# A decoder block on one core: TensorE's order in the recurrence heads written out by hand

## The chip, the cores and the metric

The kernel runs on one core of a Trainium2 chip. The metric is the time of one execution on the device in microseconds (us); a measurement is a median over several runs. The engines are TensorE (PE, with its weight loads shown apart as PEld), VectorE (DVE), ScalarE (ACT), GpSimd (POOL) and SyncE (SP), which here only issues transfers.

## What is computed

One decoder block over 1024 tokens of width 1024, all in float32. A projection gives seven parts; a gated recurrence (HGRN2, 8 heads of 128 by 128, chunks of 16 tokens in the reference) and a causal pooling over 2, 4, 8 and 16 tokens run side by side, are gated and added; then come a layer norm, an MLP with squared ReLU and a second layer norm.

```
proj = x @ w_in -> [q | f | i | og | pool_v | gate_a | gate_b]
f = lb + (1 - lb) * sigmoid(f);  k = 1 - f;  q = silu(q) / sqrt(128)
S_t = diag(f_t) S_{t-1} + k_t v_t^T;   o_t = S_t^T q_t          (v = i, per head)
a = (rms_norm(o) * g * sigmoid(og)) @ w_a
b = (causal_mean_w(pool_v) - pool_v) @ w_pool * pool_scale       (per group)
x = LN(alpha * x + (sigmoid(gate_a) * a + sigmoid(gate_b) * b) @ w_out)
x = LN(alpha * x + relu(x @ w_up)^2 @ w_down)
```

## The kernel before

Every large product runs in Strassen's manner: a pair of 128-column blocks of weights for both halves of the tokens takes seven products (p1 to p7) on sums of operands. Each operand is split into a high and a low part of type fp32r, and a product is 12 matmuls of 128x512 (`prod`, lines 201, 203 and 204). `pair` builds the seven steps, `run` goes through them: for each step it makes the weights' parts (a copy on ACT, line 118, and a subtraction on DVE, line 119, into the ring `w` of ten tiles, two for each operand), then calls the product, which drains its bank in PSUM through `takes`.

The stage of the heads follows the projection of `i` (the values). Its pairs are:

- `head_inputs(h)`, q and f of head h, kept on chip in the rings `q` and `f`;
- `output_gates(h)` (two heads at a time), stored to DRAM and loaded back as `og`;
- `pooled(g)`, whose means DVE makes in the drains, stored to DRAM (`pod`);
- `gates(j)`, eight of them, stored to DRAM (`gad`, `gbd`).

`pool_products(g)` then loads the pooled tiles back (`pod` into the tags `og` and `v`), splits them and multiplies them by `w_pool` (`mm3`, lines 105 to 107), 24 matmuls each.

The recurrence works on 16 halves: 8 heads, each with two halves of 512 tokens, a half being four chunks of 128 tokens. `hgrn(h, u, ...)` does a half. DVE scans the running products of f in blocks of 16 (`fd`, line 811), takes their reciprocal (line 817) and makes scaled queries and keys (`qc`, `kc`, `kr`, `q64`, `k64`, `qi`, `ke`). PE turns the keys (`ke`, line 870), multiplies them with the values (`ds`, line 875), from which DVE makes the states one after the other (`st`, line 883). PE makes the scores in pieces of 32 and 64 (lines 887 and 898) into the bank `sc`; DVE masks them into `att` (line 905). PE multiplies `att` with the values and `qi` with the states into `o` (lines 915 and 918). ACT squares, takes the root and scales (lines 923 to 928), PE turns the result (line 931), DVE multiplies it by the output gate (line 932) and SP's queue stores it to DRAM (`od`, line 933). `o_sums(kp)` loads four such tiles, makes the four Strassen sums and stores them.

A planner orders the instructions of each engine: it simulates a timeline and takes, on each engine, the ready instruction that was written earliest, or that stands in a block of raised priority. So PE's order in the heads comes from the plan: the narrow products of the recurrence lie wherever the plan had them ready, between the 512-wide products of the pairs. The trace order in which heads and pairs are written is the loop over `h` and `u` with the table `EXTRAS`. Every load and almost every store of the stage is issued by SP, in one queue.

Tags are rings of buffers: a tile waits until the tile that had its buffer is released, stores to DRAM included. Before, the rings are `q`=3, `f`=3, `og`=2, `v`=2, `tA`=2, `tC`=2, `st`=2, the others 1.

After `pool_products` and the last `gates`, the merged stage (`a_pair`), the output projection, the norm and the MLP follow; the change doesn't touch them.

Of the kernel before, what the change touches and what calls it, by code (L numbers as in the profile page):

```python
# [16 lines left out]
P = 128  # L17
# [12 lines left out]
PRIO_LAST = 3000  # L30
# [13 lines left out]
def tile_hybrid_block(  # L44
# [311 lines left out]

    def run(*pairs, made=(), behind=()):


        for i, steps in enumerate(zip(*pairs)):  # L360
            made_now = list(made[i]) if made else []
            if made_now:
                made_now.pop(0)()
            with tc.issue_after(made_last[behind[i]]) if behind and behind[i] else nullcontext():
                ws = [{operand: operand() for operand in operands} for operands, _ in steps]
            for n in range(len(ws[0])):
                if made_now:
                    made_now.pop(0)()
                for w, (_, products) in zip(ws, steps):
                    operand, product = products[n]  # L370
                    product(w[operand])

# [219 lines left out]
    def loaded(src, tile_of):  # L592
        t = tile_of()
        nc.sync.dma_start(out=t, in_=src)
        return t
# [9 lines left out]
    def o_sums(kp, tile_of=c_tile):  # L605

        a11, a21, a12, a22 = (loaded(od[k][u], tile_of) for k, u in ((kp, 0), (kp, 1), (kp + CH, 0), (kp + CH, 1)))
# [4 lines left out]
        for name, t in zip(("s3", "s2", "s1", "s4"), (a21, a11, a22, a12)):  # L612
            nc.sync.dma_start(out=osd[name][kp], in_=t)
# [4 lines left out]
    with tc.tile_pool(name="tmp", bufs=1, side="right", reuse_waits="tile") as tmp:  # L618
# [3 lines left out]
        att = [hgp.tile([P, CH, P], F32, name=f"att{i}") for i in range(1)]  # L622
        for t in att:
            G.memset(t, 0.0)
# [6 lines left out]
        RINGS = dict(q=3, f=3, og=2, v=2, tA=2, tC=2, st=2)  # L631
# [11 lines left out]
        def head_inputs(h, behind=()):  # L643
            fs, qs = [None, None], [None, None]
# [23 lines left out]
            return fs, qs  # L668
# [19 lines left out]
        def gates(j):  # L688
# [3 lines left out]
            def take(dst, src=None, more=None):  # L692
                def put(t):
# [5 lines left out]
                    nc.sync.dma_start(out=dst if more is None else more, in_=s)  # L699
# [8 lines left out]
        def pool_products(g):  # L708
# [6 lines left out]
            raw = raw_tile().rearrange("p k n c -> p (k n c)")[:, : 2 * 2 * P].rearrange("p (k c) -> p k c", c=2 * P)  # L715
            nc.sync.dma_start(out=raw, in_=w_pool[g].rearrange("(k p) c -> p k c", p=P))
            wh, wl = split(raw, lambda: room(F32R).rearrange("p (k c) -> p k c", c=2 * P))
            for u in range(2):
                pl = [split(loaded(pod[2 * g + i][u], room), row_tile) for i in range(2)]
                for i in range(2):  # L720
# [9 lines left out]
                    nc.sync.dma_start(out=pbd[j][u], in_=t)  # L730

        def pooled(g):
# [20 lines left out]
            def put(c, i, u):  # L753
                nc.sync.dma_start(out=pod[j + i][u], in_=c[:, HALO:])
# [51 lines left out]
        def hgrn(h, u, ft, q, v, og, state):  # L806

            fd = tt("tA")
            for i in range(2):
                w = slice(i * QUARTER, (i + 1) * QUARTER)  # L810
                V.tensor_tensor_scan(fd[:, w], starts.rearrange("p b s -> p (b s)"), ft[:, w], 1.0, ALU.max, ALU.mult)
            k = ft
            A.activation(k, ft, AF.Identity, bias=cmask[:, P - 1 : P], scale=-1.0)
            r = tt("tC")
            for i in range(CH):
                w = slice(i * P, (i + 1) * P)
                V.reciprocal(r[:, w], fd[:, w])  # L817
            T = small("T", [P, NB])
            G.tensor_copy(T, blk(fd)[:, :, SUB - 1])
            T2 = T.rearrange("p (b e) -> p b e", e=2)  # L820
            p32 = small("p32", [P, CH, 4])
            p32f = p32.rearrange("p c b -> p (c b)")
            G.tensor_mul(p32f, T2[:, :, 0], T2[:, :, 1])
            p64 = small("p64", [P, CH, 2])
            p32p = p32f.rearrange("p (b e) -> p b e", e=2)
            G.tensor_mul(p64.rearrange("p c e -> p (c e)"), p32p[:, :, 0], p32p[:, :, 1])
            dec = small("dec", [P, CH])
            G.tensor_mul(dec, p64[:, :, 0], p64[:, :, 1])
            eq = small("eq", [P, CH, 4])
            G.memset(eq[:, :, 0:1], 1.0)  # L830
            G.tensor_copy(eq[:, :, 1], p32[:, :, 0])
            G.tensor_copy(eq[:, :, 2], p64[:, :, 0])
            G.tensor_mul(eq[:, :, 3], p64[:, :, 0], p32[:, :, 2])
            ek = small("ek", [P, CH, 4])
            G.memset(ek[:, :, 3:4], 1.0)
            G.tensor_copy(ek[:, :, 2], p32[:, :, 3])
            G.tensor_copy(ek[:, :, 1], p64[:, :, 1])
            G.tensor_mul(ek[:, :, 0], p64[:, :, 1], p32[:, :, 1])


            V.tensor_mul(q, q, fd)
            kc = tt("tD")
            V.tensor_mul(kc, k, r)
            kr = tt("tE")
            V.tensor_mul(blk(kr), blk(kc), bc(T, [P, NB, SUB]))
            A.copy(pairs_of(kc)[:, :, 0], pairs_of(kr)[:, :, 0])
            qc = tt("tF")
            A.copy(pairs_of(qc)[:, :, 1], pairs_of(q)[:, :, 1])
            V.tensor_mul(
                pairs_of(qc)[:, :, 0], pairs_of(q)[:, :, 0],  # L850
                bc(pairs_of(r)[:, :, 0, SUB - 1], [P, NB // 2, SUB]),
            )
            V.tensor_mul(pairs_of(q)[:, :, 1], pairs_of(q)[:, :, 1], bc(T2[:, :, 0], [P, NB // 2, SUB]))
            V.tensor_mul(pairs_of(kr)[:, :, 0], pairs_of(kr)[:, :, 0], bc(T2[:, :, 1], [P, NB // 2, SUB]))
            q64 = hgp.tile([P, CH, 2, 32], F32, tag="q64", name=nm("q64"))
            k64 = hgp.tile([P, CH, 2, 32], F32, tag="k64", name=nm("k64"))
            A.copy(q64[:, :, 0], half64(q, 1)[:, :, 0])
            V.tensor_mul(q64[:, :, 1], half64(q, 1)[:, :, 1], bc(p32[:, :, 2], [P, CH, 32]))
            A.copy(k64[:, :, 1], half64(kr, 0)[:, :, 1])
            V.tensor_mul(k64[:, :, 0], half64(kr, 0)[:, :, 0], bc(p32[:, :, 1], [P, CH, 32]))  # L860
            qi = tt("tA")
            b32 = lambda t: t.rearrange("p (b s) -> p b s", s=32)
            V.tensor_mul(b32(qi), b32(q), bc(eq.rearrange("p c b -> p (c b)"), [P, 16, 32]))
            ke = tt("tC")
            V.tensor_mul(b32(ke), b32(kr), bc(ek.rearrange("p c b -> p (c b)"), [P, 16, 32]))


            pt = ps_tile("tr", 2)
            for c in range(CH - u):
                PE.transpose(pt[:, c * P : (c + 1) * P], ke[:, c * P : (c + 1) * P], ident)  # L870
            ket = tt("tH")
            A.copy(ket[:, : (CH - u) * P], pt[:, : (CH - u) * P])
            ds = ps_tile("hg", 2)
            for c in range(CH - u):
                PE.matmul(ds[:, c * P : (c + 1) * P], ket[:, c * P : (c + 1) * P], v[:, c], start=True, stop=True)
            st = tt("st")
            for c in range(CH - u):
                o = st[:, c * P : (c + 1) * P]
                if state is None and c == 0:
                    V.tensor_copy(o, ds[:, 0:P])  # L880
                else:
                    prev = state[:, 3 * P :] if c == 0 else st[:, (c - 1) * P : c * P]
                    V.scalar_tensor_tensor(o, prev, dec[:, c : c + 1], ds[:, c * P : (c + 1) * P], ALU.mult, ALU.add)


            def score(part, lo, keys, queries):
                PE.matmul(sc[part : part + 32, lo : lo + queries.shape[-1]], keys, queries, start=True, stop=True)

            for c in range(CH):
                for b in range(4):  # L890
                    lo = c * P + b * 32
                    score(b * 32, lo, kc[:, lo : lo + 32], qc[:, lo : lo + 32])
            for c in range(CH):
                for b in (0, 2):
                    lo = c * P + b * 32
                    score(b * 32, lo + 32, kr[:, lo : lo + 32], q[:, lo + 32 : lo + 64])
            for c in range(CH):
                PE.matmul(
                    sc[0:64, c * P + 64 : (c + 1) * P],
                    k64[:, c].rearrange("p a b -> p (a b)"),  # L900
                    q64[:, c].rearrange("p a b -> p (a b)"),
                    start=True, stop=True,
                )
            at = att[(2 * h + u) % 1]
            V.copy_predicated(
                at, cmask.bitcast(U32).unsqueeze(1).to_broadcast([P, CH, P]),
                sc.rearrange("p (c t) -> p c t", t=P),
            )


            o = ps_tile("hg", 2)
            for c in range(CH):
                w = slice(c * P, (c + 1) * P)
                first = state is None and c == 0
                PE.matmul(o[:, w], at[:, c], v[:, c], start=True, stop=first)
                if not first:
# [485 lines left out]
```

## Time and profile before

| | before |
|---|---|
| median of 3 runs | 1462.83 us (1462.3 to 1464.97) |
| profiled execution | 1460.19 us, of which the span from the first to the last instruction is 1458.5 us |
| mean granted PE clock | 0.996 |
| matmuls | 7377 |
| HBM | 154.16 MB read, 71.30 MB written, 155 GB/s over the span |

The heads stretch from about 107 us to about 650 us of the span. In the profile's rows, "<-" behind an idle time names what ended it; a line number is that of the kernel; an engine's name with a "q" behind it stands for the queue that issues transfers. [...]

### The profile page before, as it was taken

To read this page: it belongs to the slowest core of one execution; us is meant where nothing else is said; L and a number is where in the kernel's file an instruction comes from. 1 tells how busy PE (TensorE), PEld (TensorE's weight loads), DVE (VectorE), ACT (ScalarE), POOL (GpSimd) and SP (SyncE) were. 2 spreads that over 40 slices of the span, in tenths; PEclk is the share of its full clock that TensorE was granted. 3 is DMA by queue.
4 is the path that set the end of the run, shared out by engine and by line. 5 is a ranking of instruction groups with operands and counts; after the bars stand their busy time and mean duration, and the time that the engine had idled before them with its cause. 6 is when DMAs were issued, how large, how long until landed. Compare 5 with 4: busy or idle time off the path is not lost.

```text
span 1458.5 us, 20662 instructions
## 1 busy us (share of the span) xinstructions
PE 1436.4 (98%) x7377; PEld 1187.9 (81%) x7377; DVE 1141.6 (78%) x1838; ACT 758.3 (52%) x1383; POOL 58.6 (4%) x244
## 2 busy tenths in 40 slices
PE   8999999999999998999999999999999999999997
PEld 7888888888888886788888878888888888888886
DVE  5967989899898885768985597666666787777977
ACT  5445565666656655556542376555555443333535
POOL 0001001001000010000002100000000100000000
PEclk9999999999999999999999999999999999999999
DMA  7232233323234447897672225444474874445322
GB/s 253 70 126 87 85 98 101 109 75 114 90 99 138 152 132 249 301 299 241 223 247 99 73 94 195 159 146 144 152 261 149 275 260 150 153 141 163 130 73 116
DMA packets 160615, 226.82 MB, mean 156 GB/s; under 512 B 11232, under 2 KB 84480, under 8 KB 160512
## 3 DMA queue, kind: packets, MB, share of 16 engines
q1 hardware_dynamic: 158576, 218.93, 44.7%
q0 software_dynamic: 1152, 4.19, 0.8%
q10 hardware_dynamic: 784, 2.38, 0.5%
q8 instruction: 58, 0.95, 0.3%
q14 instruction: 45, 0.37, 0.1%
HBM read 154.16 MB, written 71.30 MB: 155 GB/s over the span
## 4 chain that ended last, share of the span: by engine, by line
PE 94%; DVE 3%; DMA 1%; ACT 1%; issue 0%; SPq 0%; DVEq 0%
PE ps_pj L201 16%; PE ps_pj L203 16%; PE ps_pj L204 16%; PE ps_pj L1283 4%; PE ps_pj L1285 4%; PE ps_pj L1284 4%; PE ps_pj L106 3%; PE ps_pj L107 3%; PE ps_pj L105 2%; PE ps_tr L1285 1%; PE ps_tr L1283 1%; PE ps_tr L1284 1%; PE ps_sc L201 1%; PE ps_sc L203 1%; PE ps_sc L204 1%; PE ps_hg L203 1%
## 5 line engine op out<-in xcount | busy, mean ns | idle before, releaser
L201 PE MATMUL ps_pj<-act,w 128*128 128x512 f32 x1068 | 421.6, 395 | 0.4 <-ACT act L123 0.2
L203 PE MATMUL ps_pj<-act,w 128*128 128x512 f32 x1068 | 415.1, 390 | 0.5 <-DVE act L124 0.5
L204 PE MATMUL ps_pj<-act,w 128*128 128x512 f32 x1068 | 414.1, 390 | 0.0
L201 PEld LDWEIGHTS ps_pj<-act,w 128*128 128x128 f32 x1068 | 200.6, 188 | 42.8 <-ACT act L123 0.6
L204 PEld LDWEIGHTS ps_pj<-act,w 128*128 128x128 f32 x1068 | 200.5, 188 | 42.3
L203 PEld LDWEIGHTS ps_pj<-act,w 128*128 128x128 f32 x1068 | 200.6, 188 | 40.6 <-DVE act L124 0.9
L118 ACT CAST w<-t 128x512 fp32r<-128x512 f32 x170 | 104.7, 620 | 105.0 <-PE ps_pj L203 53.8
L118 ACT CAST w<-raw 128x512 fp32r<-128x512 f32 x143 | 88.2, 620 | 117.3 <-PE ps_pj L203 62.5
L119 DVE TENSOR_TENSOR w<-raw,w 128x512 fp32r<-128x512 f32 x143 | 99.8, 702 | 55.2 <-ACT w L118 53.9
L119 DVE TENSOR_TENSOR w<-t,w 128x512 fp32r<-128x512 f32 x170 | 115.9, 685 | 29.6 <-ACT w L118 29.4
L1245 ACT CAST act<-act 128x1024 fp32r<-128x1024 f32 x66 | 66.9, 1050 | 107.9 <-issue 35.0
L1246 DVE TENSOR_TENSOR act<-act,act 128x1024 fp32r<-128x1024 f32 x66 | 79.3, 1220 | 18.5 <-ACT act L1245 15.8
L1285 PE MATMUL ps_pj<-act,act 128*128 128x512 f32 x240 | 92.9, 389 | 0.0
L1284 PE MATMUL ps_pj<-act,act 128*128 128x512 f32 x240 | 92.9, 389 | 0.0
L1283 PE MATMUL ps_pj<-act,act 128*128 128x512 f32 x240 | 92.4, 389 | 0.0
L275 DVE TENSOR_TENSOR c<-c,ps_pj 128x512 f32<-128x512 f32 x95 | 64.5, 681 | 18.0 <-PE ps_pj L204 13.4
L271 ACT COPY c<-ps_pj 128x512 f32<-128x512 f32 x96 | 55.2, 582 | 12.8 <-PE ps_pj L204 12.8
L817 DVE RECIPROCAL tC<-tA 128x128 f32<-128x128 f32 x64 | 54.1, 904 | 0.0
L1284 PEld LDWEIGHTS ps_pj<-act,act 128*128 128x128 f32 x240 | 45.1, 188 | 9.4
L1285 PEld LDWEIGHTS ps_pj<-act,act 128*128 128x128 f32 x240 | 45.1, 188 | 9.4
L1283 PEld LDWEIGHTS ps_pj<-act,act 128*128 128x128 f32 x240 | 45.1, 188 | 9.3
L241 DVE TENSOR_TENSOR t<-raw,raw 128x512 f32<-128x512 f32 x43 | 29.6, 689 | 21.9 <-DMA raw<-in_w_in_dram 19.7
(415 smaller groups left out, 2719.8 us busy)
## 6 DMA issues: line engine op xcount, KB each, us to landing
h<-c SPq DMA_DIRECT2D x106, 256.0 KB, 2.1
act<-h SPq DMA_DIRECT2D x78, 256.0 KB, 2.9
raw<-in_w_in_dram SPq DMA_DIRECT2D x64, 256.0 KB, 3.4
draw<-in_w_down_dram SPq DMA_DIRECT2D x16, 1024.0 KB, 7.8
raw<-in_w_up_dram SPq DMA_DIRECT2D x30, 512.0 KB, 4.2
raw<-in_w_in_dram SPq DMA_DIRECT2D x18, 512.0 KB, 4.0
hf<-h SPq DMA_DIRECT2D x34, 256.0 KB, 2.9
c<-o SPq DMA_DIRECT2D x24, 256.0 KB, 3.4
```

The source lines that it names most:

```text
L118: A.copy(hi, src)
L119: V.tensor_sub(lo, src, f(hi))
L201: PE.matmul(ps, wh[:, k], th, start=first and k == 0, stop=False, skip_group_check=True)
L203: PE.matmul(ps, wh[:, k], tl, start=False, stop=False, skip_group_check=True)
L204: PE.matmul(ps, wl[:, k], th, start=False, stop=k == CH - 1, skip_group_check=True)
L271: A.copy(t, ps)
L275: V.tensor_add(t, t, ps)
L1245: A.copy(hi, src)
L1246: V.tensor_sub(lo, src, f(hi))
L1283: PE.matmul(ps, hh[:, w], wh, start=fresh and n == 0, stop=False, skip_group_check=True)
L1284: PE.matmul(ps, hh[:, w], wl, start=False, stop=False, skip_group_check=True)
L1285: PE.matmul(ps, hl[:, w], wh, start=False, stop=n == M - 1, skip_group_check=True)
```

## The change

1. All products on PE from the first `output_gates` to the last `gates` stand in a block in which PE keeps the order in which they are written (`manual_schedule` for PE). The other engines are planned as before.
2. The recurrence is rewritten as a class `Half` with its pieces and a generator `recurrence()`, which `run` advances by one turn after each product of a pair. A half gets 8.5 turns. Its narrow products stand in two groups: at a half's first turn the outputs of the half before (`outputs`), the turning of its own keys and all its scores (`turn_keys`, `scores`); four turns later the turning of the outputs of the half before and its own states (`turn_outputs`, `states`). `prepare` (DVE's and ACT's work for the next half) is spread over the other turns. The table `ORDER` replaces `EXTRAS`: 147 products from `output_gates(0)` to `gates(5)`, behind them the turns that are left, then `pool_products(0)`, `gates(6)`, `pool_products` 1, 2 and 3, `gates(7)`.
3. In `prepare` the reciprocal of all 512 running products goes; instead two scans that run backwards over f give the products to the end of a block, and the reciprocal is taken of the 32 block ends alone.
4. Stores of `gates` and `output_gates` go to ACT's queue; stores of the outputs, of the pooled tiles, of `pool_products`, and loads and stores of `o_sums`, go to POOL's.
5. Rings: `og` 2 to 1, `tC` 2 to 1, `f` 3 to 4, `tH` 1 to 2. The weights of `w_pool` are loaded into `tA` and no longer into the ring of the large weights. `o_sums` follow the last half of a head in the recurrence.

The diff, cut to its core:

```diff
-PRIO_LAST = 3000
+PER_HALF = 8.5
+TURN_BACK = 4
+TURNS_AHEAD = 3
+ORDER = (
+    ("inputs", 1), ("pooled", 0), ("inputs", 2), ("gates", 0), ("output_gates", 2), ("inputs", 3), ("pooled", 1),
+    ("inputs", 4), ("output_gates", 4), ("gates", 1), ("inputs", 5), ("pooled", 2), ("inputs", 6), ("output_gates", 6),
+    ("gates", 2), ("inputs", 7), ("pooled", 3), ("gates", 3), ("gates", 4), ("gates", 5),
+)
...
     def run(*pairs, made=(), behind=()):
...
                     product(w[operand])
+                    next(turning[0], None)
...
     def o_sums(kp, tile_of=c_tile):
-        a11, a21, a12, a22 = (loaded(od[k][u], tile_of) for k, u in ((kp, 0), (kp, 1), (kp + CH, 0), (kp + CH, 1)))
+        a11, a21, a12, a22 = (loaded(od[k][u], tile_of, nc.gpsimd) for k, u in ((kp, 0), (kp, 1), (kp + CH, 0), (kp + CH, 1)))
...
-            nc.sync.dma_start(out=osd[name][kp], in_=t)
+            nc.gpsimd.dma_start(out=osd[name][kp], in_=t)
...
-        RINGS = dict(q=3, f=3, og=2, v=2, tA=2, tC=2, st=2)
+        RINGS = dict(q=3, f=4, og=1, v=2, tA=2, tH=2, st=2)
...
-                    nc.sync.dma_start(out=dst, in_=s)
+                    nc.scalar.dma_start(out=dst, in_=s)
...
-                    nc.sync.dma_start(out=dst if more is None else more, in_=s)
+                    (nc.scalar if more is None else nc.gpsimd).dma_start(out=dst if more is None else more, in_=s)
...
-            raw = raw_tile().rearrange("p k n c -> p (k n c)")[:, : 2 * 2 * P].rearrange("p (k c) -> p k c", c=2 * P)
+            raw = tt("tA").rearrange("p (k c) -> p k c", c=2 * P)
...
-                    nc.sync.dma_start(out=pbd[j][u], in_=t)
+                    nc.gpsimd.dma_start(out=pbd[j][u], in_=t)
...
-                nc.sync.dma_start(out=pod[j + i][u], in_=c[:, HALO:])
+                nc.gpsimd.dma_start(out=pod[j + i][u], in_=c[:, HALO:])
...
+            def prepare(self):
+                h, u = self.h, self.u
+                ft, q = inputs[h][0][u], inputs[h][1][u]
+                fd = tt("tA")
+                for i in range(2):
+                    w = slice(i * QUARTER, (i + 1) * QUARTER)
+                    V.tensor_tensor_scan(fd[:, w], first_of, ft[:, w], 1.0, ALU.max, ALU.mult)
+                to_end = tt("tC")
+                G.memset(to_end[:, HALF - 1 :], 1.0)
+                yield
+                V.tensor_tensor_scan(
+                    to_end[:, HALF - 2 : QUARTER - 1 : -1], ft[:, HALF - 1 : QUARTER : -1], first_of[:, 1:],
+                    1.0, ALU.mult, ALU.max,
+                )
+                V.tensor_tensor_scan(
+                    to_end[:, QUARTER - 1 :: -1], ft[:, QUARTER : 0 : -1], first_of, 0.0, ALU.mult, ALU.max,
+                )
+                k = ft
+                A.activation(k, ft, AF.Identity, bias=cmask[:, P - 1 : P], scale=-1.0)
+                rT = small("rT", [P, NB])
+                V.reciprocal(rT, blk(fd)[:, :, SUB - 1])
...
+                yield
+                V.tensor_mul(q, q, fd)
+                self.kr = kr = tt("tE")
+                V.tensor_mul(kr, k, to_end)
+                yield
...
+            def outputs(self):
+                self.og = loaded(ogd[self.h][self.u], lambda: tt("og"))
+                o = ps_tile("hg", 2)
...
+            def turn_outputs(self):
+                pt = ps_tile("tr", 2)
+                for c in range(CH):
+                    PE.transpose(pt[:, chunk(c)], self.on[:, chunk(c)], ident)
+                V.scalar_tensor_tensor(self.og, pt, g_col[:, self.h : self.h + 1], self.og, ALU.mult, ALU.mult)
+                nc.gpsimd.dma_start(out=od[self.h][self.u], in_=self.og)
+
+        def recurrence():
...
+            now, old, at = half(0, None), None, 0.0
+            now.load()
+            for _ in now.prepare():
+                yield
+            for _ in range(TURNS_AHEAD):
+                yield
+            for n in range(2 * HEADS + 1):
+                if old:
+                    old.outputs()
+                if now:
+                    now.turn_keys()
+                    now.scores()
+                yield
+                if now:
+                    now.far_queries()
+                nxt = half(n + 1, now) if now else None
+                pieces = nxt.prepare() if nxt else iter(())
+                at += PER_HALF
+                for turn in range(1, round(at) - round(at - PER_HALF)):
+                    if turn == TURN_BACK:
+                        if old:
+                            old.turn_outputs()
+                        if now:
+                            now.states()
+                        if nxt:
+                            nxt.load()
+                        if old and old.u and old.h >= CH:
+                            last = old.h == HEADS - 1
+                            tags = iter(("tD", "tE", "tF", "tC"))
+                            o_sums(old.h - CH, (lambda: tt(next(tags))) if last else c_tile)
+                    else:
+                        next(pieces, None)
+                    yield
+                for _ in pieces:
+                    pass
+                now, old = nxt, now
+
+        inputs = [None] * HEADS
+        head_inputs(0, (None, None, "p6", None, None))
+        with tc.manual_schedule(engines={mybir.EngineType.PE}):
+            turns = turning[0] = recurrence()
+            output_gates(0)
+            for what, j in ORDER:
...
+            for _ in turns:
+                pass
+            for what, j in (
+                ("pool_products", 0), ("gates", 6), ("pool_products", 1), ("pool_products", 2), ("pool_products", 3), ("gates", 7),
+            ):
+                dict(gates=gates, pool_products=pool_products)[what](j)
```

More of the change, by code (lines that the diff above doesn't have):

```diff
@@ L621, in tile_hybrid_block @@
         G.memset(starts[:, :, 0:1], 1.0)
-        att = [hgp.tile([P, CH, P], F32, name=f"att{i}") for i in range(1)]
-        for t in att:
-            G.memset(t, 0.0)
+        att = hgp.tile([P, CH, P], F32, name="att")
+        G.memset(att, 0.0)
         hg_tags.remove("sc")
@@ L804, in bc @@
             return a.unsqueeze(len(a.shape)).to_broadcast(shape)
[L806 to L880, printed above, removed]
-                else:
[L882 to L916, printed above, removed]
-                    prev = state[:, 3 * P :] if c == 0 else st[:, (c - 1) * P : c * P]
-                    PE.matmul(o[:, w], qi[:, w], prev, start=False, stop=True)
-            ss = small("ss", [P, CH])
-            on = tt("tH")
-            for c in range(CH):
-                w = slice(c * P, (c + 1) * P)
-                A.activation(on[:, w], o[:, w], AF.Square, accum_out=ss[:, c : c + 1])
-            A.activation(ss, ss, AF.Sqrt, bias=eps_rms, scale=1.0 / P)
-            V.reciprocal(ss, ss)
-            for c in range(CH):
-                w = slice(c * P, (c + 1) * P)
-                A.activation(on[:, w], o[:, w], AF.Copy, scale=ss[:, c : c + 1])
-            pt = ps_tile("tr", 2)
-            for c in range(CH):
-                PE.transpose(pt[:, c * P : (c + 1) * P], on[:, c * P : (c + 1) * P], ident)
-            V.scalar_tensor_tensor(og, pt, g_col[:, h : h + 1], og, ALU.mult, ALU.mult)
-            nc.sync.dma_start(out=od[h][u], in_=og)
-            return st
@@ L946, in tile_hybrid_block, with chunk @@
[L946 to L962 removed]
+        def chunk(c):
+            return slice(c * P, (c + 1) * P)
```

149 lines of the change are left out of this document (119 added, 30 removed).

## The prediction

> **What bounds the kernel now.** I read the page first, then what TensorE (PE) waits for, then stage windows and the timeline of the one place where it stops.
>
> ```profile
> span 1458.5 us, 20662 instructions
> PE 1436.4 (98%) x7377; PEld 1187.9 (81%) x7377; DVE 1141.6 (78%) x1838; ACT 758.3 (52%) x1383; POOL 58.6 (4%) x244
> PE 94%; DVE 3%; DMA 1%; ACT 1%; issue 0%; SPq 0%; DVEq 0%
> ...
> PE ps_pj L105 <- ACT w L118: 4.7, 1, 4.7
> ...
> PE ps_hg L915 <- DVE st L883: 1.2, 1, 1.2
> PE ps_pj L106 <- DVE w L119: 0.8, 1, 0.8
> ...
> 300.00:350.00 50.00, 50.00 (x348) 41.72 (x347) 48.96 (x100) 33.24 (x76) 4.50 (x26) 1.00 0.30 95
> 550.00:600.00 50.00, 43.25 (x252) 34.83 (x252) 28.76 (x52) 24.34 (x57) 0.00 (x0) 0.93 0.77 254
> ```
>
> PE is busy for 98% of the span and carries 94% of the chain. In the heads (about 107 to 650 us) it never stops before 575 us, though VectorE (DVE) is full at 48.96 of 50 us in the worst window. So nothing that makes DVE, ScalarE (ACT) or a queue faster is worth anything there by itself. Two things can be won: PE time spent on breaks between kinds of product, and the hole near 580 us.
>
> ```profile
> 574.10 0.83 PE L875 MATMUL ps_hg<-v,tH 128*128 128x128 f32 x6
> 577.80 0.39 PE L918 MATMUL ps_hg<-st,tA 128*128 128x128 f32 x2
> 582.85 1.22 PE L105 MATMUL ps_pj<-w,q 128*128 128x512 f32 x2 [4.66 <-ACT w L118]
> 591.31 0.40 PE L107 MATMUL ps_pj<-w,f 128*128 128x512 f32 x1
> 592.45 0.39 PE L201 MATMUL ps_pj<-act,w 128*128 128x512 f32 x1
> ...
> 582.80:586.00 3.20, 3.11 (x7) 1.95 (x8) 1.57 (x3) 3.13 (x7) 0.00 (x0) 0.50 0.78 265
> 586.00:589.40 3.40, 3.40 (x13) 2.62 (x12) 1.24 (x2) 2.80 (x5) 0.00 (x0) 0.61 0.30 77
> ```
>
> Five 512-wide products start between 591.31 and 592.45: 0.227 us each at full clock. From 574.10 to 582.85 PE had 2.5 us of work in 8.75, so 6.2 us are lost. From 582.85 to 592.45 it ran 22 such products and four transposes, 5.4 us of work in 9.6: 4.2 us lost, 0.8 of them a wait, some 3.3 to the granted clock (0.50, then 0.61). **The hole costs 10.4 us.** [...]
>
> **The change, part by part.**
>
> *Groups.* The timeline gives what narrow products cost, as the time between the 512-wide rows around them less the two 0.227 us that those take.
>
> ```profile
> 137.96 0.38 PE L887 MATMUL sc<-tF,tD 128*32 128x32 f32 x18
> ...
> 588.71 0.49 PE L931 MATMUL ps_tr<-ident,tH 128*128 128x128 f32 x3
> ...
> 436.20 0.39 PE L204 MATMUL ps_pj<-act,w 128*128 128x512 f32 x1
> 436.43 0.60 PE L931 MATMUL ps_tr<-ident,tH 128*128 128x128 f32 x4
> 437.53 0.40 PE L203 MATMUL ps_pj<-act,w 128*128 128x512 f32 x1
> ...
> 442.53 0.40 PE L204 MATMUL ps_pj<-act,w 128*128 128x512 f32 x1
> 442.76 1.05 PE L875 MATMUL ps_hg<-v,tH 128*128 128x128 f32 x8
> 445.35 0.39 PE L203 MATMUL ps_pj<-act,w 128*128 128x512 f32 x1
> ...
> 450.36 0.39 PE L204 MATMUL ps_pj<-act,w 128*128 128x512 f32 x1
> 450.58 0.60 PE L915 MATMUL ps_hg<-v,att 128*128 128x128 f32 x4
> 452.38 0.40 PE L203 MATMUL ps_pj<-act,w 128*128 128x512 f32 x1
> ```
>
> Here one half's work stands nearly whole: both transposes 0.88, states with all scores 2.37, outputs 1.57: 4.81 us. Second halves turn one chunk less, first halves have one product fewer, which makes 76.3 us for 16 whole halves. Added up in this way, the 67 interruptions of before (first and last shown) come to 81.4 us without the hole. The surplus is breaks inside the scores. Two whole groups per half: **−5.1 us**. Nothing else of PE's work changes: no product is added or removed.
>
> *DVE and ACT in `prepare`.*
>
> ```profile
> L817 DVE RECIPROCAL tC<-tA 128x128 f32<-128x128 f32 x64 | 54.1, 904 | 0.0
> L811 DVE TENSOR_TENSOR_SCAN tA<-starts,f 128x256 f32<-128x256 f32 x32 | 20.3, 672 | 1.1 <-PE ps_hg L918 1.1
> L843 DVE TENSOR_TENSOR tD<-f,tC 128x512 f32<-128x512 f32 x16 | 10.9, 683 | 0.0
> ...
> ACT w L118 <- PE ps_pj L203: 56.6, 43, 4.3
> ```
>
> Each half loses four reciprocals (3.6 us) and one 512-wide multiplication (0.7); it gains two scans (1.3), half a multiplication and a small reciprocal (about 0.6 as I estimate): about −2.4 us, 38 us in all. PE never waited for DVE in the heads, so I count it at 0; it is the slack that the fixed order lives on.
>
> *The written order.* PE can no longer step past a product whose operand is late; behind it every later product queues. ACT's wait for L203 says that weight parts are made as early as PE frees their buffers, so in steady state they are ready. The drains keep their 2.7 us (12 products) between two products of a pair. Before, waits outside the hole were near 0; the only late recurrence operand cost 1.2 us. Between 0 and 10 us over 34 groups I take **+3 us**, near the low end.
>
> *Stores on ACT's and GpSimd's (POOL's) queues.* SP's queue loses some 130 stores; nobody on PE waited for SP outside the hole, so 0. ACT gets about 46 issues, POOL about 80, on an engine busy for 4%; what they queue behind is the gate's sigmoid on ACT and the small decay products on POOL, which have a half's time.
>
> *The hole.* The last half's outputs now come after the fifth of the seven products of `gates(5)`; its way back (`turn_outputs`) falls behind the last product, and the next thing in PE's order is `pool_products(0)`. Its first operand is a pooled tile loaded into tag `og`, a ring that goes from two buffers to one: the load waits until the last half's own output is stored. `gates(6)`, which could fill the time, is written behind. So the hole stays. Its chain:
>
> ```profile
> 565.13 0.28 ACT L923 ACTIVATE tH<-ps_hg 128x128 f32<-128x128 f32 x1 [0.93 <-PE ps_hg L918]
> 566.29 1.28 ACT L924 ACT_TABLE_LOAD   x1
> 569.99 1.14 ACT L928 ACTIVATE tH<-ps_hg,ss 128x128 f32<-128x128 f32 x4 [2.10 <-DVE ss L925]
> 571.55 0.75 DVE L932 SCALAR_TENSOR_TENSOR og<-ps_tr,prm,og 128x512 f32<-128x512 f32 x1 [0.24 <-PE ps_tr L931]
> 582.18 0.62 ACT L118 CAST w<-og 128x512 fp32r<-128x512 f32 x1 [2.75 <-DMA og<-po]
> 582.83 0.69 DVE L119 TENSOR_TENSOR w<-og,w 128x512 fp32r<-128x512 f32 x1 [0.38 <-ACT w L118]
> ...
> o<-og SPq DMA_DIRECT2D x16, 256.0 KB, 2.1
> og<-og SPq DMA_DIRECT2D x16, 256.0 KB, 2.8
> og<-po SPq DMA_DIRECT2D x8, 256.0 KB, 3.9
> ...
> L1293 POOL DMA_DIRECT2D act<-x x7 | 3.9, 559 | 331.0 <-DVE c L275 324.2 <-PE ps_pj L204 6.3
> ```
>
> The norm takes 3.9 us of work on ACT (565.13 to 571.13 less the 2.1 idle) against two products (5.4 us) left on PE: 0.3 us of waiting. Then scaling 0.75, POOL's issue 0.56, store 2.1, load 3.3 (between 2.8 and 3.9), cast 0.62, hops 0.5: **8.1 us** idle, between 6.8 (shortest rows, no hops) and 11 (a slower store, gates' sigmoids first). The clock falls as before: **+3.3**. [...]
>
> *The ring afterwards.* `pool_products` 1 to 3 now stand back to back, each with two loads into the single `og` buffer. One turn of it is load 3.3, cast 0.62, rest 0.69, hops 0.3: 4.9 us, against 2.7 us of PE work. The first two are hidden by `gates(6)` (7 products, 19 us); the later ones put PE behind by 0.2, 2.2 and 2.2: **+4.6 us**, between 0 and 8.
>
> Sum: −5.1 − 10.4 + 8.1 + 3.3 + 4.6 + 3.0 = +3.5 us. The profiled execution took 1460.19 us (span 1458.5), so 1463.7 there; the median of before lies 2.64 higher, which gives 1466.3.
>
> **The rivals.**
>
> *The hole shrinks and the ring is hidden* (faster). With 6.8 and 3.3 and no other waits the sum is −5.4 us: 1457.4. For it: after `prepare` was cut, DVE and ACT have room, and loads no longer queue behind stores on SP. Against it: every row of the chain is a median already and `og` has one buffer. It decides once the terms 8.1, 4.6 and 3.0 come out more than 6.4 us lower together.
>
> *ACT's bursts stop PE* (much slower). Squares from 565.13, a table load of 1.28 and the root stand together on ACT for 2.7 us; a copy of 0.6 behind them makes the next product of the same bank, 2.7 us away, 0.6 late, and sigmoids load a table back. Once a half, 16 × 0.6 = 10 us more: 1476. Against it: before had the same bursts and PE did not wait.
>
> [...]
>
> *The written order changes nothing on PE* (the hole and the breaks as before): 1462.8.
>
> **How the numbers follow.** Forecast 0.50, faster rival 0.34, ACT 0.08, POOL 0.03, nothing 0.05. A measurement of this kernel can tell about 0.2% (2.9 us) from no change. The forecast's own range, 1461 to 1474, holds a third of its chance within that; of the faster rival 0.30 is beyond it. So faster 0.30, same 0.26 (0.17, 0.04 and 0.05), slower 0.44 (0.33, 0.08 and 0.03). The range goes from the faster rival with a little more off its waits, 1455.5, to the forecast with ACT's bursts, 1476.
>
> **What would show it.** Right: 34 interruptions of PE, about 76 us; a PE wait of 7 to 11 us at the first L105 for ACT's cast of `og`, with a granted clock near 0.5 behind it; two or three waits of 1 to 2.5 us at later L105; DVE's busy time 30 to 40 us lower. Wrong: no wait at the first L105, or many waits of over 0.5 us at L203 and L204 inside the heads.

## The result, and the profile after

The changed kernel takes **1480.76 us** (median of 4 runs, 1479.85 to 1482.52) against 1462.57 us for the kernel before beside it: a ratio of 1.0125 [1.0113, 1.0138], 18.2 us slower. The forecast was 1466.3 us with a range of 1455.5 to 1476: slower, as forecast, but by 18 us and not by 4, and outside the range. The profiled execution took 1480.14 us. All times here are of executions at a granted clock of 0.988 or more; one slow execution of experiment 5 (its profiled one, 2428 us at a clock of 0.556) and one of experiment 12 (1603 us) are left out.

The page of the changed kernel: busy time, the chain by engine, the dearest rows of PE and of the drains.

```profile
span 1478.2 us, 20742 instructions
...
PE 1437.6 (97%) x7377; PEld 1190.5 (81%) x7377; DVE 1112.9 (75%) x1822; ACT 760.0 (51%) x1383; POOL 127.4 (9%) x342
...
PE 81%; DVE 6%; issue 5%; DMA 5%; ACT 1%; POOL 1%; SPq 0%; DVEq 0%; POOLq 0%; ACTq 0%
...
L208 PE MATMUL ps_pj<-act,w 128*128 128x512 f32 x1068 | 420.7, 395 | 14.3 <-ACT c L278 10.2
...
L278 ACT COPY c<-ps_pj 128x512 f32<-128x512 f32 x96 | 55.9, 583 | 14.5 <-DMA s<-c 7.4
```

PE has the same 7377 matmuls and about the same busy time, but its share of the chain fell from 94% to 81%: DVE, DMA and issues now stand in the chain. The last two rows already tell where: the first matmul of a product (L208; L201 before) waited 10.2 us for copies of PSUM banks by ACT (L278), and those copies waited 7.4 us for a transfer `s<-c`. That is a store of `o_sums`, which no step of the prediction priced.

What PE waits for in the changed kernel (total, times, longest):

```profile
PE ps_pj L208 <- ACT c L278: 10.2, 3, 8.5
PE ps_pj L112 <- ACT w L125: 7.2, 1, 7.2
PE ps_pj L114 <- DVE f L126: 2.1, 2, 1.3
PE ps_pj L208 <- ACT f L278: 1.8, 1, 1.8
PE ps_pj L112 <- ACT q L125: 1.7, 1, 1.7
...
PE ps_pj L208 <- DVE c L282: 1.0, 1, 1.0
```

The second row is the hole, as forecast (7 to 11 us, then at L105; L112 is the same line). The third and fifth belong to the pooled products. The first, fourth and last are waits inside the heads, where before PE never stopped for longer than 0.24 us ahead of 575 us.

Windows of the changed kernel (length, busy time of PE, PEld, DVE, ACT and POOL, then granted clock, DMA share, GB/s):

```profile
400.00:450.00 50.00, 47.83 (x287) 39.73 (x286) 43.28 (x95) 26.26 (x53) 11.64 (x27) 1.00 0.42 137
...
554.00:565.00 11.00, 2.85 (x13) 2.04 (x11) 7.84 (x18) 1.50 (x3) 3.07 (x6) 0.77 0.69 231
565.00:568.60 3.60, 3.28 (x8) 2.61 (x9) 1.14 (x2) 0.89 (x2) 0.17 (x1) 0.50 0.76 280
...
607.00:614.60 7.60, 0.40 (x4) 0.16 (x2) 0.87 (x2) 1.96 (x4) 1.09 (x2) 0.78 0.49 173
614.60:618.00 3.40, 3.40 (x8) 2.30 (x9) 3.30 (x6) 0.36 (x1) 1.10 (x3) 0.50 0.44 124
```

There are two long stops, one at 556 us and one at 607 us, and behind each the granted clock is 0.50. The one at 607 us is the hole that the prediction worked out. This is the one at 556 us, in the timeline of the changed kernel (start, duration, in brackets the idle time before and what ended it):

```profile
540.57 1.14 POOL L603 DMA_DIRECT2D c<-o  x2 [1.01 <-ACT tH L971]
...
550.77 0.55 POOL L603 DMA_DIRECT2D c<-o  x1 [9.06 <-ACT w L125]
...
552.26 0.55 POOL L763 DMA_DIRECT2D po<-c  x1 [0.40 <-DVE st L950]
...
556.46 0.39 PE L211 MATMUL ps_pj<-act,w 128*128 128x512 f32 x1
...
558.05 0.55 POOL L603 DMA_DIRECT2D c<-o  x1 [5.24 <-DMA po<-c]
...
561.25 0.69 DVE L617 TENSOR_TENSOR c<-c,c 128x512 f32<-128x512 f32 x1 [2.99 <-DMA c<-o]
...
562.24 0.54 POOL L622 DMA_DIRECT2D s<-c  x1 [3.64 <-DVE c L617]
...
564.68 0.59 ACT L278 COPY c<-ps_pj 128x512 f32<-128x512 f32 x1 [7.40 <-DMA s<-c]
...
565.32 0.80 PE L208 MATMUL ps_pj<-act,w 128*128 128x512 f32 x1 [8.47 <-ACT c L278]
```

Read it from below. PE waits for ACT to copy out a bank; the copy goes into a tile `c`; that tile is held by `o_sums` until its store (L622) has landed. `o_sums` takes four `c` tiles (there are six, in two rings of two and four) and got them one by one: two loads at 540.57, the third at 550.77, the fourth at 558.05, when a pooled tile had been stored (`po<-c`). Only then could DVE make the sums. The drains of `gates` and `pooled` need tiles of the same rings. PE's order is fixed, so nothing was put in the place of the product that could not drain. The two groups of `o_sums` ahead of it (loads from 414.5 and 483.9 us) held their tiles for 20 us and more as well, and PE made no stop of over 2 us; why it was the third is not shown.

### The profile page after: what moved, and what is told of

Same layout as the page of the kernel before. It is cut to its first block, busy times and chain, and to the rows that moved or that the text cites. A ratio compares the mean times of both kernels' runs of the same rounds, so it can differ in the third digit from the quotient of the medians.

```text
span 1478.2 us, 20742 instructions
## 1 busy us (share of the span) xinstructions
PE 1437.6 (97%) x7377; PEld 1190.5 (81%) x7377; DVE 1112.9 (75%) x1822; ACT 760.0 (51%) x1383; POOL 127.4 (9%) x342
## 4 chain that ended last, share of the span: by engine, by line
PE 81%; DVE 6%; issue 5%; DMA 5%; ACT 1%; POOL 1%; SPq 0%; DVEq 0%; POOLq 0%; ACTq 0%
PE ps_pj L208 13%; PE ps_pj L210 13%; PE ps_pj L211 13%; PE ps_pj L1360 4%; PE ps_pj L1359 4%; PE ps_pj L1361 4%; PE ps_pj L114 2%; PE ps_pj L112 2%; PE ps_pj L113 2%; PE ps_tr L1360 1%; PE ps_tr L1359 1%; PE ps_tr L1361 1%; PE ps_sc L208 1%; PE ps_sc L211 1%; PE ps_sc L210 1%
## 5 line engine op out<-in xcount | busy, mean ns | idle before, releaser
L208 PE MATMUL ps_pj<-act,w 128*128 128x512 f32 x1068 | 420.7, 395 | 14.3 <-ACT c L278 10.2
L208 PEld LDWEIGHTS ps_pj<-act,w 128*128 128x128 f32 x1068 | 201.0, 188 | 59.8 <-ACT c L278 11.5
L125 ACT CAST w<-t 128x512 fp32r<-128x512 f32 x170 | 105.5, 622 | 141.2 <-PE ps_pj L210 90.8
L125 ACT CAST w<-raw 128x512 fp32r<-128x512 f32 x143 | 88.6, 623 | 128.7 <-PE ps_pj L210 81.5
L278 ACT COPY c<-ps_pj 128x512 f32<-128x512 f32 x96 | 55.9, 583 | 14.5 <-DMA s<-c 7.4
L1225 ACT ACTIVATE c<-c 128x512 f32<-128x512 f32 x61 | 38.6, 633 | 1.7
```

The lines of the kernel that those rows point to most:

```text
L125: A.copy(hi, src)
L208: PE.matmul(ps, wh[:, k], th, start=first and k == 0, stop=False, skip_group_check=True)
L278: A.copy(t, ps)
```

## The experiments

The theory after this reading: **a tile ring (a tag's set of buffers) that runs empty stops a written order for as long as the tile is held**, at 556 us through `c` and `o_sums`, at 607 us through `og`. Rivals: POOL's queue is what makes the loads and stores late; the single place of `gates(6)` is wrong; the written order costs this much by itself. A time is the median, a ratio stands to the kernel before on the same chip (1462.4 to 1463.0 us). All edits are to the changed kernel unless it is said otherwise.

**1. `o_sums` back on SyncE's queue**

```diff
-        a11, a21, a12, a22 = (loaded(od[k][u], tile_of, nc.gpsimd) for ...)
+        a11, a21, a12, a22 = (loaded(od[k][u], tile_of) for ...)
...
-            nc.gpsimd.dma_start(out=osd[name][kp], in_=t)
+            nc.sync.dma_start(out=osd[name][kp], in_=t)
```

> As the changed kernel, but the loads and stores of o_sums go through SP's queue again instead of POOL's. Theory A (the 8.6 us stop of PE near 556 us comes from the c ring: o_sums takes four of its six tiles one after the other, the gates' copy waits for one of them, and PE, whose order is written, waits for the copy): the stop stays, 0 to 2 us shorter, time 1478 to 1482 us. Rival B (the stop comes from POOL's queue, where each transfer waits behind the others): the stop and the low clock behind it go, about 12 us less, 1468 to 1470 us.

1479.69 us, 1.0113 [1.0098, 1.0128]. The stop is still there; the timeline of this kernel:

```profile
548.77 0.37 SPq L603 DMA_DIRECT2D c<-o  x1
...
555.24 0.32 SPq L603 DMA_DIRECT2D c<-o  x1
...
558.74 2.50 SPq L622 DMA_DIRECT2D s<-c  x4
...
562.92 0.80 PE L208 MATMUL ps_pj<-act,w 128*128 128x512 f32 x1 [8.08 <-ACT c L278]
```

With another queue the last two tiles still come 6.5 us apart, and PE stands 8.08 us, as theory A has it. The queue isn't the cause.

**2. `o_sums` out of the heads.** The four calls stand behind the last turn of the recurrence, on the tiles `tD`, `tE`, `tF`, `tC`, which are free then.

```diff
-                        if old and old.u and old.h >= CH:
-                            ...
-                            o_sums(old.h - CH, (lambda: tt(next(tags))) if last else c_tile)
...
             for _ in turns:
                 pass
+            for kp in range(CH):
+                tags = iter(("tD", "tE", "tF", "tC"))
+                o_sums(kp, lambda: tt(next(tags)))
```

> As the changed kernel, but all four o_sums stand behind the last turns of the recurrence and take tD, tE, tF, tC instead of c tiles; the queue stays POOL's. Theory A (c ring): the stop near 556 us and the clock's fall behind it go, some of the smaller waits too, 10 to 13 us less, 1468 to 1471 us. Rival B (POOL's queue) expects the same here, so this run alone doesn't part them. Rival C (the stop is due to ACT or DVE being late with the gates' work itself): the stop stays, 1479 to 1482 us.

1474.23 us, 1.0078 [1.0063, 1.0093]: 6.5 us less, where 10 to 13 were expected. The stop at 556 us is gone, and the hole has grown, in the waits of PE of this kernel:

```profile
PE ps_pj L112 <- ACT w L125: 11.5, 1, 11.5
```

The sums' transfers now run beside the last half's store and the load behind it. The store's issue comes 3.6 us ahead of the load's (599.36 and 602.98 us) where it was 2.7 us in the changed kernel, and from the load to the cast that reads it 5.3 us pass (to 608.28) where it was 2.7. Some 4 us of what was won are given back there.

**3. `gates(6)` ahead of the first pooled products**, to fill the hole.

```diff
-                ("pool_products", 0), ("gates", 6), ("pool_products", 1), ...
+                ("gates", 6), ("pool_products", 0), ("pool_products", 1), ...
```

> As the changed kernel, but gates(6) stands ahead of pool_products(0) in PE's order. If the hole at 607 us is the chain of the last half's output through og as predicted, seven products cover it: the 7.2 us wait and the 3.3 us of low clock go, while the four pool_products in a row lose 2 to 4 us more on the og ring: 1472 to 1476 us. If the hole is due to something that gates(6) needs as well (weights, w tiles), it moves and the time stays at 1479 to 1482 us.

1481.67 us, 1.0127 [1.0109, 1.0145]: nothing won. The time is the rival's, but the mechanism is the theory's, with more lost on the pooled products than the 2 to 4 us that it gave. The hole at 607 us is gone; the four pooled groups then follow each other with nothing between them, and PE's steps there are 3.6, 1.7 and 5.2 us long. In the timeline of this kernel, the first of these waits and the two casts that it hangs on:

```profile
633.21 0.62 ACT L125 CAST w<-og 128x512 fp32r<-128x512 f32 x1 [2.80 <-DMA og<-po]
...
634.25 0.61 ACT L125 CAST q<-tA 128x512 fp32r<-128x512 f32 x1
...
634.92 0.80 PE L112 MATMUL ps_pj<-w,q 128*128 128x512 f32 x1 [3.19 <-ACT q L125]
```

PE waits for the cast of the next group's weights (`q<-tA`), which stands in ACT's queue behind a cast of `og` that waited 2.80 us for its load. So one `og` tile for eight loads cost the same wherever the filler stood.

**4. Two buffers for `og`, and `f` back to three**

```diff
-        RINGS = dict(q=3, f=4, og=1, v=2, tA=2, tH=2, st=2)
+        RINGS = dict(q=3, f=3, og=2, v=2, tA=2, tH=2, st=2)
```

> As the changed kernel, but the rings are og=2 and f=3, as before the change, instead of og=1 and f=4. If the single og buffer makes both the hole at 607 us and the waits of the later pool_products, both go nearly: 12 to 16 us less, 1465 to 1469 us. If f=3 makes the heads' scans late under the written order, new waits of several us at the groups appear before 550 us and the time is 1475 us or more. If og is not the cause, 1479 to 1482 us.

1470.79 us, 1.0052 [1.0037, 1.0067]: 10.0 us less, where 12 to 16 were expected. PE's waits in this kernel:

```profile
PE ps_pj L208 <- ACT c L278: 9.7, 3, 7.7
PE ps_pj L112 <- DVE q L738: 2.2, 1, 2.2
```

The 7.2 us wait for `w` (L125) is no longer in the list, the `c` wait stays at 7.7. The fourth `f` buffer bought nothing in the heads: the short waits there are as long as before the edit, to 0.4 us. At the pooled products there are still waits, now for DVE's L738, which empties the bank by multiplying it with the loaded `gbd` tile (tag `q`): there the name `og` in the prediction was only part of the matter.

**5. TensorE planned again**, with everything else of the change kept.

```diff
-        with tc.manual_schedule(engines={mybir.EngineType.PE}):
+        with nullcontext():
```

> As the changed kernel in everything (classes, turns, queues, rings, the new scans), but PE's order is left to the planner again. Theory A (a written order makes PE stand wherever one operand waits for a buffer: c near 556 us, og near 607 us and in the pool products): PE steps past these products, most of the 8.6 + 3.3 us near 556 us and of the 5.7 us of small waits go, while the hole shrinks little and the groups break up again (up to 5 us back): 1462 to 1470 us. Rival (the rings, queues and the new trace order are themselves too tight, whatever PE's order): 1476 to 1482 us.

1472.30 us (three runs), 1.0065 [1.0048, 1.0082]: 8.5 us less than the changed kernel. Expected was 1462 to 1470, so less came back than I thought. So some 8.5 us of the 18 go with the written order itself; the other 9.6 stay when PE is planned, with the rings and the order of the trace as in the changed kernel. Only the time says so: where these 9.6 us lie was not read from a trace.

**6. Experiments 2 and 4 together** (`og` two, `o_sums` late), and **7. the same with one `o_sums` behind `gates(6)` and behind each of the next three pooled groups**.

> Both repairs in one: og=2 and f=3, and the four o_sums behind the last turns on tD, tE, tF, tC. Alone they brought 10.0 and 6.5 us; alone the second made the hole 4 us longer, which og=2 should undo. Theory A expects them to add up to 14 to 20 us: 1460 to 1467 us, without a wait of over 3 us in the heads. If they share a cause, 1467 to 1471 us.

> As the kernel with both repairs, but the four o_sums stand one each behind gates(6) and the pool_products 1, 2, 3, so that they do not crowd the place behind the last turn. If the crowd costs there, 1 to 4 us less than with both repairs alone; if o_sums late make the merged stage wait for the sums (they are loaded at its third step), some us more.

1464.88 us, 1.0011 [1.0001, 1.002], and 1464.42 us, 1.0016 [1.0006, 1.0025]. The two edits add up, nearly: 6.5 and 10.0 us alone, 15.9 together. Where `o_sums` stands among the last stages makes no difference, once it is out of the heads and the hole is closed. PE's waits in experiment 6:

```profile
PE ps_pj L112 <- DVE q L738: 3.8, 1, 3.8
PE ps_tr L977 <- ACT tH L971: 2.6, 1, 2.6
```

**8. TensorE planned again in experiment 6.** If the rings are the cause, the written order should now cost little.

> The version of 1464.9 us (og two deep, o_sums behind the last turns) with TensorE's order left to the planner, the other engines' edits kept. Theory (with the long stops cured, the written order gives its 5 us of groups and takes about as much in small stops): 1461 to 1467. Rival A (the written order still costs the 8 us that it cost in the changed kernel): 1455 to 1459. Rival B (it is worth more than its groups once the rings are right): 1468 to 1475.

1466.38 us, 1.0027 [1.0017, 1.0038]. In experiment 5 the planner was 8.5 us better than the written order; here it is 1.5 us worse, with intervals that overlap. The theory's figure (1461 to 1467) holds: what the written order cost came through the rings. The repairs are worth 15.9 us under the written order and 5.9 under the planner's, so the tight rings cost something under either. The 4 us that are left against the kernel before with both repairs and a planned PE are open.

**9. The turn back later** (`PER_HALF` 8.25, `TURNS_AHEAD` 5, in experiment 6): the last half's outputs come two products earlier to the turning (four products' time instead of two), against the 2.6 us wait at L977.

> og two deep, o_sums behind the last turns (the version of 1464.9 us), and PER_HALF 8.25 with TURNS_AHEAD 5: the last half's outputs behind product 143 and its turn back behind product 147, so that ScalarE has four products' time for tH before the transposes read it. Theory (each stop of a written order is worth its length, and a long one the slow clock behind it too): the 2.98 us step ahead of the transposes goes, nothing takes its place, 1460 to 1463. Rival (the wait is ScalarE's work itself, and only moves to the first pooled products): 1464 to 1466, with a wait at the first pooled products longer by 2 to 3 us.

1466.73 us, 1.0038 [1.0022, 1.0054]: nothing won; the seven runs lie between 1464.7 and 1472.1 us, and the median is a little above the rival's 1464 to 1466. L977 no longer waits, but PE's waits in this kernel have

```profile
PE ps_pj L208 <- ACT c L278: 3.3, 5, 1.4
PE ps_pj L112 <- ACT q L125: 2.6, 1, 2.6
```

The first row is five short waits spread from 207 to 570 us, in a written order that has shifted. The second comes at 630.9 us, at the third group of pooled products, where it was 0.6 us in experiment 6: there the rival's 2 to 3 us turned up, two groups later than it said. The cast that PE waits for stands in ACT's queue behind four casts of `og` and `v` tiles, and ahead of three of them ACT itself waited 0.6 to 0.9 us for their loads. So ACT's own work is not all of it.

**10. As 9, with the loads of G' and B' on GpSimd's queue**, against the 3.8 us wait for L738.

```diff
-                    t = room() if j == KT - 1 else loaded(gbd[j][u], room)
+                    t = room() if j == KT - 1 else loaded(gbd[j][u], room, nc.gpsimd)
```

> As both_turns, and the loads of G' and B' in pool_products (tag q) issued by GpSimd's queue rather than SyncE's, where they stand behind loads of the stage that follows. Theory: the 3 to 4 us step at the second pooled products, which waits for a VectorE product with q, goes to under 1 us, and the time falls by another 1 to 4 us: 1457 to 1462. Rival (q's ring of three is what makes the load late, not the queue): the step stays at 3 us, and the time is that of both_turns within 1 us.

1470.87 us, 1.0061 [1.0044, 1.0078]: 4 us worse than experiment 9 by the medians, with intervals that overlap; neither the theory nor the rival gave this time. The wait for L738 is as long as before (3.7 us), and the wait ahead of it is still there (2.4 us, after 2.6). A `c` wait inside the heads, at 570.8 us, has grown from 1.4 to 3.3 us. The timeline of this kernel at the pooled products:

```profile
638.86 0.55 POOL L603 DMA_DIRECT2D q<-gb  x1 [0.70 <-issue]
640.65 0.55 POOL L603 DMA_DIRECT2D f<-gb  x1 [1.24 <-issue]
643.14 0.55 POOL L603 DMA_DIRECT2D q<-gb  x1 [1.94 <-issue]
646.14 0.55 POOL L603 DMA_DIRECT2D f<-gb  x1 [2.46 <-PE ps_pj L114]
...
649.52 0.47 PE L112 MATMUL ps_pj<-w,q 128*128 128x512 f32 x1 [3.68 <-DVE q L738]
```

The loads come 1.8 to 3.0 us apart on an engine with little else to do, the last one when PE has freed an operand. So SyncE's queue was not what held them. That speaks for the rival's cause, the rings `q` and `f` that loads and operands share; a longer ring was not run.

**11. The kernel before with the new `prepare` alone**, and **12. the kernel before with the moved queues alone** (items 3 and 4 of the change).

> The kernel before with one part of the change alone: the backward scans in place of the 512-wide reciprocals, planned order, rings and queues as before. The prediction counted these 30 to 40 us of VectorE's time at nothing, since PE never waited for VectorE there: 1460 to 1465 us, and VectorE's busy time 30 to 40 us lower. If VectorE's load had set the planner's order and so the breaks or the hole, 1452 to 1458 us.

> The kernel before with the moved queues alone: gates from ScalarE's queue, outputs, sums, pooled G', B' and pooled tiles from GpSimd's. Theory (the queues are worth nothing by themselves, since what waits is a tile or a planner's slot): 1461 to 1465. Rival (GpSimd's stores land later and hold og, or ScalarE's issues push its drains): 1466 to 1470. Rival on the other side (SyncE's queue was what the planner's groups waited for): 1455 to 1460.

1464.75 us, 1.0015 [1.0005, 1.0024], and 1463.15 us, 1.0002 [0.9992, 1.0012]. The page of the first:

```profile
PE 1439.4 (98%) x7377; PEld 1190.2 (81%) x7377; DVE 1112.5 (76%) x1822; ACT 757.6 (52%) x1383; POOL 82.6 (6%) x260
```

It saves 29.1 us of DVE's time against before (1141.6) and is no faster, if anything 2 us slower. The second moves nothing. Neither part is worth anything by itself, or costs more than 2 us, with PE planned; under the written order only the queue of `o_sums` was tried (experiment 1).

No version beats the kernel before: of those with the written order, experiments 6 and 7 come within 0.11% and 0.16% of it.

## Why the prediction was wrong in size, step by step

Times between the starts of PE's rows, less the 0.227 us of a full-speed product (in the profile its row is 0.39 us long, and the next starts 0.227 us after it, so steps are read from start to start); the predicted terms stand against the profiled executions.

| term | predicted, us | measured, us |
|---|---|---|
| groups (67 interruptions to 34) | -5.1 | -5.5 (81.4 to 75.9) |
| hole of before gone | -10.4 | -10.4 |
| hole after: idle and clock | 8.1 + 3.3 | 7.4 + 2.6 |
| pooled products behind it | 4.6 | 5.0 |
| written order's waits | 3.0 (0 to 10) | 16.8 |
| stages behind the heads | 0 | 1.7 |
| sum | 3.5 | 17.6 |

The first product of the MLP, behind which both kernels run alike, starts 18.9 us later than before (853.33 against 834.43 us), so the table leaves 1.3 us. A third stretch of low clock behind the pooled products, which the table does not hold, is about that: from 659.0 to 662.4 us PE's products come 0.427 us apart, 1.6 us in all. Of the 2.6 us behind the hole, 0.6 are a late operand at 619.9 us.

**Right: the groups.** 34 interruptions take 75.9 us, forecast 76.3. This is a sound way to price an order: count the narrow products' time between two full-speed rows. The windows show its limit: in 400 to 450 us PE is busy for 47.83 of 50 us, and what the groups gain is spent beside them.

**Right: the hole.** The chain in the changed kernel:

```profile
607.34 0.75 DVE L978 SCALAR_TENSOR_TENSOR og<-ps_tr,prm,og 128x512 f32<-128x512 f32 x1 [2.27 <-PE ps_tr L977]
...
608.38 0.55 POOL L979 DMA_DIRECT2D o<-og  x1 [16.12 <-DVE og L978]
...
611.11 4.43 SPq L603 DMA_DIRECT2D og<-po  x2
...
613.83 0.62 ACT L125 CAST w<-og 128x512 fp32r<-128x512 f32 x1 [5.18 <-DMA og<-po]
...
614.50 0.80 PE L112 MATMUL ps_pj<-w,q 128*128 128x512 f32 x1 [7.20 <-ACT w L125]
```

Scaling, POOL's issue, store, load, cast: the links are those of the sum, and the stop is 7.4 us against 8.1. The load took 2.7 us where 3.3 were priced, and the 0.3 us ahead of the turning did not come. Experiment 4 took the single `og` buffer away and the hole with it. From POOL's queue this store has a median of 2.6 us, where it had 2.1 us from SyncE's before; the view of the DMA issues of the changed kernel has it, and in the same view the twelve stores `s<-c` of the same size and queue have a median of 3.7:

```profile
o<-og POOLq DMA_DIRECT2D x16, 256.0 KB, 2.6
```

**Right in size, not wholly in cause: the pooled products.** 5.0 us against 4.6, in four waits of 1.9, 1.0, 0.6 and 1.5 us where 0.2, 2.2 and 2.2 were forecast. All four are for the casts and differences that make an operand, and experiment 4 left waits there, for the `q` and `f` rings. It was not `og` alone, and that the sum comes out within 0.4 us is in part luck.

**Right: DVE and the queues at 0**, as far as it was tried: experiment 1 under the written order, 11 and 12 with PE planned. DVE's busy time fell by 28.7 us, a little less than the 30 to 40 forecast. The 0.03 for POOL (slower) did not come true: its issues to its queue took 0.54 to 0.57 us on average in each kind of transfer, where the seven `act<-x` of before took 0.56.

**Failed: "The written order", +3 us.** It measured 16.8: at 556 us 8.6 of stop and 2.4 of the lower clock behind it, and five short waits (at 129, 172, 425, 430 and 510 us) that make 5.8. The prediction priced operands that PE reads: weights made early, a late state of 1.2 us. It did not price the other side of a product, the tile into which its bank is drained. The change puts `o_sums` behind the states of a half, and so in front of drains that take `c` tiles from the same rings; the tiles for its four loads come free one by one. The list of the change has this among the rings, and the prediction gave it no term. Its sign of being wrong looked in the same place: in the heads no product waited at what were L203 and L204; the waits came at the first matmul of a product (L208, once L201), and they were for its bank to be emptied. PE's waits of before did not show the term, but the timeline of the SP queue of before did, for a reader who asked how long a group of `c` tiles is held:

```profile
446.09 0.44 SPq L594 DMA_DIRECT2D c<-o  x1
...
485.25 0.39 SPq L594 DMA_DIRECT2D c<-o  x1
...
488.88 0.32 SPq L613 DMA_DIRECT2D s<-c  x1
```

From the first load of a group to its first store 43 us passed, and PE did not wait in that time. That the planner put other products in the place of those that could not drain is the likely reason, and is not shown. Also, the lower clock was charged for the hole alone.

**The rivals.** "ACT's bursts stop PE" is what three of the short waits are (at 172, 425 and 510 us), smaller than priced: 4.0 us in three places and not 10 in sixteen. The other two are for DVE (1.7 us). At 425 us in the changed kernel ACT waits at the head of its queue for a scan of the new `prepare`, with the copy of a bank queued behind it:

```profile
424.50 0.73 ACT L845 ACTIVATE f<-f,cmask 128x512 f32<-128x512 f32 x1 [3.06 <-DVE tC L841]
...
426.68 0.58 ACT L278 COPY f<-ps_pj 128x512 f32<-128x512 f32 x1
...
427.32 0.50 PE L208 MATMUL ps_pj<-act,w 128*128 128x512 f32 x1 [1.77 <-ACT f L278]
```

So there the burst is a wait for DVE more than ACT's own work. At 510 us it is ACT's own, as the rival had it: ACT worked for all but 0.8 of the 7 us ahead. Moving the scans in the turns was not tried. "The hole shrinks" is refuted by the 7.2 us; "the written order changes nothing" by the rows above.

## What to carry to other kernels

Before an engine's order is fixed by hand, list for each instruction not only what it reads but where its result goes: every ring that a drain takes a tile from, who else takes tiles from it, and until which store. A group of tiles that is taken one by one from a shared ring (four of six here) belongs behind the fixed stretch or on tiles of its own; that and one more `og` buffer gave 15.9 of the 18.2 us back. A saving on an engine beside the path (29 us of VectorE) and a moved queue were worth nothing here, and of the groups' 5.5 us the times show at most the 1.5 us between experiments 8 and 6.

## What the runs showed of the hardware that was not expected

Behind a wait of PE of 2.6 us the granted clock was 0.50, and once behind two waits of 1.8 us together. Windows of experiment 6, behind the 2.6 us wait for L977 and the 3.8 us wait for L738:

```profile
598.70:602.10 3.40, 3.40 (x9) 2.62 (x8) 1.03 (x2) 2.93 (x5) 1.11 (x3) 0.50 0.84 201
641.00:646.40 5.40, 5.33 (x13) 4.20 (x14) 2.61 (x4) 0.88 (x2) 2.17 (x4) 0.50 0.97 309
```

And one of the changed kernel, behind the short waits at the pooled products:

```profile
659.00:662.40 3.40, 3.40 (x9) 2.65 (x8) 2.44 (x4) 2.30 (x5) 0.54 (x1) 0.50 0.88 311
```

In the kernel before, the clock was 1.00 from 576.0 to 578.5 us, behind the 1.2 us wait for `st`, and 0.50 from 582.8 to 586.0 us, behind the 4.7 us wait for `w`. Behind the wait of 2.6 us in experiment 6 PE's products came 0.427 us apart for 3.4 us. Behind a step of 2.1 us in the changed kernel, at 646.8 us, they did not (the clock is 1.00 from 649.0 to 655.0 us); but from 659.0 us on they did, where the waits were 0.5 us (at 656.2) and 1.3 us (at 658.2). So the length of a single stop does not decide it here; what does is not shown. Beside their length these stops cost 1.6 to 2.6 us of slow products: 1.7 behind 2.6 us, 1.6 behind the two short waits, 2.6 behind 3.8, and in the changed kernel 1.9 behind 7.2 and 2.4 behind 8.5.
